# Gram products of an RWKV layer on four array tiles, with the transposes as identity products and a longer lead for their operands

## The chip, the core and the metric

One core of a Trainium2 chip runs the whole step: TensorE (PE, its weight loads as PEld), VectorE (DVE), ScalarE (ACT), GpSimd (POOL) and SyncE (SP), which issues most DMAs. The metric is device time in microseconds. The granted clock of TensorE has two levels, 1.2 and 2.4 GHz, shown as 0.5 and 1.0.

## What is computed

One inference step of a hybrid layer over 1024 latent and 256 context tokens: RMSNorm with adaptive modulation, one input projection, eight heads of differential attention, sixteen heads of a bidirectional RWKV-7 scan, gates, an output projection, a final RMSNorm. The part that the change touches is the scan, per head and direction:

```python
def step(S, inp):
    r_t, w_t, k_t, v_t, kk_t, b_t = inp
    sa = jnp.einsum('bhvk,bhk->bhv', S, -kk_t)
    S = S * w_t[:, :, None, :] + sa[..., None] * b_t[:, :, None, :] + v_t[..., None] * k_t[:, :, None, :]
    return S, jnp.einsum('bhvk,bhk->bhv', S, r_t)
```

## The kernel before

**Two stages.** First come the projections: 66 column blocks of 128, each over 1280 tokens in three pieces of 512, 512 and 256. `chunk` (L327 to L335) is one such piece: 24 matmuls (L331 to L333, the high and low parts of the split operands), one evacuation, and then one `next` on each generator in `active`, which is how all other work of this stage is handed out: one step of a generator per projection piece. Then comes the mixing stage (`mix_phase`), which runs the chunked scan, the attention and the output projection.

**The scan in chunks of 32 tokens.** For each pair of heads p (eight pairs, two heads of 64 channels on partitions 0 to 63 and 64 to 127) and each direction d, `b_k` calls `decays` and `weights` for the decay factors and then `products`, which goes through the 1280 tokens in five segments of eight chunks. For a segment, `operands` (L458 to L479) writes `ra` (DVE, L469 and L470), sends it to DRAM, and writes `bk` (DVE L474 and L475, POOL L476 to L478). `gram` (L440 to L456) then makes, for every chunk and head, the 64x64 Gram product of `bk` and `ra` (L446: 16 products, on the two array tiles on the diagonal, partitions 0 to 63 to outputs 0 to 63 and 64 to 127 to 64 to 127), masks it into `km` (DVE, L447), transposes `bk` with four 128x128 transposes (L450), copies these into `km` (ACT, four copies, L453) and sends `km` to DRAM array `kt` with two DMAs (L455). There are 8 x 2 x 5 = 80 such grams. An f32 product that is not a transpose shows as two matmul records in the trace, a transpose as one.

**Buffers.** `bk` and `km` have one buffer each, `ra` has two. The PSUM pool `psm` has four banks and serves all small products of the stage. A tile `wcs` of 2560 bytes per partition keeps chunk decays of all pairs until `b_inv` sends it to DRAM at the end.

**What sets the order.** A scheduler orders each engine's instructions by its own estimate of when their inputs are there, so a gram can stand later in PE's order than where the program issues it. Each engine then runs its order strictly. `products` issues gram c one segment behind its operands:

```python
        def products(p, d, r, k, kn, wx, td, ta):
            last = None
            for c0 in range(0, T // CH, NC):
                if last is not None:
                    gram(p, d, *last)
                last = operands(p, d, r, k, kn, wx, td, ta, c0)
                yield
                if c0 == 0:
                    yield
            gram(p, d, *last)
```

**Later places that the text speaks of.** After the last pair, `b_inv` inverts small triangular blocks on POOL (L731, L733); their result goes out by the DMA at L735. The mixing stage begins with a load of `wc` on POOL's queue (L838). In the mixing stage each step has products at L875 (four per lane, on two 32-column array tiles in turn) and at L916 (eight, on four 32-column tiles); in PE's order there is a place where the four of L875 stand ahead of the eight of L916. L643 makes 32 products with 128x32 array tiles, four tiles side by side over the same 128 rows, in the projection stage.

## Time and profile before

| | |
|---|---|
| median of three runs | 2570.79 us (2562.2 to 2574.7) |
| the profiled execution | 2570.32 us, of it a span of 2568.6 us |
| PE busy | 2399.3 us, 93% of the span |
| DVE, ACT, POOL busy | 1541.7, 1282.3, 1159.6 us |
| mean granted clock of TensorE | 0.959 |
| chain that ended last | PE 64%, DMA 14%, DVE 7%, POOL 5% |

The shares are means over both stages. The projection stage ends near 1238 us; a row of a stage tells more than a row of the whole span. Time that an engine spends idle counts only where nothing else is on the path.

### The profile page before, as it was taken

To read this page: it belongs to the slowest core of one execution; us is meant where nothing else is said; L and a number is where in the kernel's file an instruction comes from. 1 tells how busy PE (TensorE), PEld (TensorE's weight loads), DVE (VectorE), ACT (ScalarE), POOL (GpSimd) and SP (SyncE) were. 2 spreads that over 40 slices of the span, in tenths; PEclk is the share of its full clock that TensorE was granted. 3 is DMA by queue.
4 is the path that set the end of the run, shared out by engine and by line. 5 is a ranking of instruction groups with operands and counts; after the bars stand their busy time and mean duration, and the time that the engine had idled before them with its cause. 6 is when DMAs were issued, how large, how long until landed. Compare 5 with 4: busy or idle time off the path is not lost.

```text
span 2568.6 us, 61542 instructions
## 1 busy us (share of the span) xinstructions
PE 2399.3 (93%) x23907; PEld 1921.9 (75%) x23907; DVE 1541.7 (60%) x3304; ACT 1282.3 (50%) x2932; POOL 1159.6 (45%) x1705
## 2 busy tenths in 40 slices
PE   5999999999999999999799999899899999999976
PEld 4888888888888888787577777677677777777754
DVE  5666675546445655533477776456674667655568
ACT  3334443334334433321377776567665577555732
POOL 4244343242433433447457778567582122321245
PEclk9999999999999999999799989999898999999987
DMA  7455656565555564566979797977889777776583
GB/s 244 110 154 132 187 145 174 136 166 161 157 145 150 134 180 120 149 168 174 227 158 194 141 183 172 203 166 166 181 193 225 193 184 169 194 197 154 143 265 114
DMA packets 477092, 437.35 MB, mean 170 GB/s; under 512 B 157288, under 2 KB 392868, under 8 KB 471681
## 3 DMA queue, kind: packets, MB, share of 16 engines
q1 hardware_dynamic: 473008, 424.74, 66.2%
q0 software_dynamic: 2704, 8.16, 1.5%
q8 instruction: 188, 3.08, 0.5%
q14 instruction: 104, 0.84, 0.1%
q10 hardware_dynamic: 1088, 0.52, 0.1%
HBM read 258.82 MB, written 163.47 MB: 164 GB/s over the span
## 4 chain that ended last, share of the span: by engine, by line
PE 64%; DMA 14%; DVE 7%; POOL 5%; SPq 4%; issue 3%; ACT 3%; POOLq 0%; DVEq 0%; ACTq 0%
PE sc L1061 6%; PE po L1115 5%; PE bank L889 3%; PE pg L446 3%; PE pa L1100 3%; PE bank L875 3%; PE pso L1284 2%; PE pso L1285 2%; PE pso L1286 2%; PE yb L795 2%; PE yb L916 2%; PE ptk L450 2%; DMA y<-ys 1%; PE psg_v L331 1%; PE psg_v L332 1%
## 5 line engine op out<-in xcount | busy, mean ns | idle before, releaser
L1061 PE MATMUL sc<-ka,q 128*128 128x512 f32 (+1 forms) x832 | 288.4, 441 | 16.9 <-DVE pb L1064 12.1
L1072 ACT ACTIVATE pb<-pb,mn 128x1536 f32<-128x1536 f32 (+1 forms) x160 | 218.3, 1365 | 55.3 <-DVE pb L1064 53.5
L904 DVE TENSOR_TENSOR R<-bank,wc 64x128 f32<-64x128 f32 x608 | 174.7, 287 | 113.8 <-PE bank L889 90.5
L1064 DVE TENSOR_SCALAR_CACHE_REDUCE pb<-sc,mn 128x512 f32<-128x512 f32 x256 | 191.6, 748 | 79.8 <-PE sc L1061 70.8
L1115 PE MATMUL po<-vk,aT 128*128 128x128 f32 x1600 | 236.3, 286 | 0.9 <-ACT aT L1102 0.9
L1115 PEld LDWEIGHTS po<-vk,aT 128*128 128x128 f32 x1600 | 210.6, 195 | 19.8 <-ACT aT L1102 1.9
L879 ACT COPY R<-bank 32x128 f32<-32x128 f32 x640 | 164.5, 257 | 120.2 <-PE bank L875 99.9
L476 POOL TENSOR_SCALAR ta<-ta,ka 128x256 f32<-128x256 f32 x80 | 81.6, 1020 | 295.0 <-DVE bk L474 294.8
L453 ACT COPY km<-ptk 64x256 f32<-64x256 f32 x320 | 117.3, 367 | 185.6 <-PE ptk L450 160.6
L731 POOL TENSOR_TENSOR tmp<-aw,tt 128x31 f32<-128x31 f32 (+15 forms) x310 | 166.8, 538 | 74.4 <-DMA aw<-kt 27.8
L733 POOL TENSOR_TENSOR tt<-tt,tmp 128x31 f32<-128x31 f32 (+15 forms) x310 | 182.3, 588 | 18.1
L1092 DVE SCALAR_TENSOR_TENSOR pb<-pb,cc,pb 128x512 f32<-128x512 f32 (+1 forms) x208 | 169.9, 864 | 2.2
L1061 PEld LDWEIGHTS sc<-ka,q 128*128 128x128 f32 x832 | 136.2, 197 | 45.4 <-DVE pb L1064 15.9
L799 ACT COPY L<-yb 32x384 f32<-32x384 f32 x312 | 146.3, 469 | 43.3 <-PE yb L795 36.7
L447 DVE TENSOR_TENSOR km<-pg,msk 128x512 f32<-128x512 f32 x80 | 55.0, 687 | 176.3 <-PE pg L446 156.6
L889 PE MATMUL bank<-R,L 128*64 128x64 f32 x2560 | 150.2, 242 | 9.7 <-ACT R L879 7.2
L889 PEld LDWEIGHTS bank<-R,L 128*64 128x64 f32 x2560 | 107.2, 144 | 69.4 <-issue 25.3
L875 PE MATMUL bank<-R,L 96*32 96x64 f32 x2560 | 133.9, 234 | 15.9 <-DVE R L904 8.5
L1284 PE MATMUL pso<-wohi,ohi 128*128 128x512 f32 x320 | 136.2, 426 | 12.4 <-DVE y L1353 7.7
L1100 PE MATMUL pa<-ident,pb 128*128 128x128 f32 x800 | 134.4, 289 | 10.9 <-DVE acc L1278 7.1
L875 PEld LDWEIGHTS bank<-R,L 96*32 96x32 f32 x2560 | 87.8, 115 | 71.8 <-issue 29.9
L1102 ACT COPY aT<-pa 128x512 f32<-128x512 f32 (+1 forms) x208 | 116.4, 569 | 37.7 <-PE pa L1100 34.1
(355 smaller groups left out, 6446.1 us busy)
## 6 DMA issues: line engine op xcount, KB each, us to landing
kt<-km SPq DMA_DIRECT2D x160, 256.0 KB, 3.7
L<-kt SPq DMA_DIRECT2D x80, 512.0 KB, 6.8
acc<-acc SPq DMA_DIRECT2D x50, 512.0 KB, 3.9
ra<-ra SPq DMA_DIRECT2D x160, 128.0 KB, 2.6
L<-ra SPq DMA_DIRECT2D x80, 256.0 KB, 6.8
R<-vb SPq DMA_DIRECT2D x160, 64.0 KB, 6.9
y<-ys SPq DMA_DIRECT2D x76, 128.0 KB, 5.8
wa<-w_ada SPq DMA_DIRECT2D x8, 1024.0 KB, 10.7
```

Of the source, the lines that this page charges most:

```text
L731: e.tensor_tensor(mv, aw[:n, t, t + 1:CH].unsqueeze(2).broadcast_to([n, w, j]), tt[:n, t:t + 1, 0:j].broadcast_to([n, w, j]), op=ALU.mult)
L733: e.tensor_tensor(tt[:n, t + 1:CH, 0:j], tt[:n, t + 1:CH, 0:j], mv, op=ALU.add)
L875: nc.tensor.matmul(bank[x][u:u + 32, 64 * d:64 * d + 64], L[0:96, h, d, k, 96:128], R[0:96, k, d, 64 * h:64 * h + 64], start=True, stop=Tr ...
L889: nc.tensor.matmul(bank[x][64 * h:64 * h + 64, o_:o_ + 64], L[:, h, d, k, 0:64], R[:, k, d, 64 * h:64 * h + 64], start=True, stop=True, ti ...
L904: nc.vector.tensor_tensor(dst[:, :, hs], bank[x][hs, 256:384].rearrange("p (d v) -> p d v", d=2), wcs[p][hs, sg + 1, :, c:c + 1].broadcast ...
L1061: nc.tensor.matmul(sc, q[:, v, m, qc], ka[:, m, 0:kn], start=(v == 0), stop=(v == 1))
L1064: nc.vector.tensor_scalar(pm[:, c * 512:c * 512 + kn], sc, -0.125, mn[:, c - 1:c] if c else None, op0=ALU.mult, op1=ALU.min, accum_out=mn[ ...
L1072: nc.scalar.activation(v, v, AF.Exp, bias=mn[:, c:c + 1], scale=-1.0, accum_out=B["l3"][:, m, k:k + 1])
L1092: nc.vector.scalar_tensor_tensor(a, B["p"][1][:, v], B["cc"], a, op0=ALU.mult, op1=ALU.add)
L1100: nc.tensor.transpose(pt[:, t * P:(t + 1) * P], B["p"][0][:, 512 * c + t * P:512 * c + (t + 1) * P], ident)
L1115: nc.tensor.matmul(po, B["aT"][c][:, t * P:(t + 1) * P], vk[:, t, :], start=(c == 0 and t == 0), stop=(c == last and t == nt - 1))
L1284: nc.tensor.matmul(ps, ohi[:, k - k0, :], whi[:, k, c], start=(n == 0), stop=False)
```

## The change

Four things. (1) The 16 Gram products and four transposes of a gram become 32 products of 64x64: for each chunk and head one with the identity (this gives the transposed `bk`) and one with `ra`, both with the same weights. They run on all four 64x64 array tiles: the first four chunks (f = 0) on the diagonal tiles, the last four (f = 1) on the other two, with outputs in two PSUM banks `pg[0]` and `pg[1]`. The four products of a tile position stand in this order: tile (0,0) identity and Gram, tile (64,64) both, tile (0,64) both, tile (64,0) both. (2) The evacuation goes by halves f: two masked products on DVE, two copies on ACT over 128 partitions, four DMAs. (3) `bk` gets two buffers, and a gram is issued two segments behind its operands: the operands of segments 1 to 4 are issued one projection piece earlier, the grams at the same pieces as before. (4) `wcs` becomes a tile of 320 bytes per pair, sent to DRAM once per pair, and the one DMA in `b_inv` goes.

```diff
@@ -311,7 +311,7 @@
 
         pr = p1.enter_context(ExitStack())
         rp = pr.enter_context(tc.tile_pool(name="rp", bufs=1, side="right", reuse_waits="tile"))
-        wcs = rp.tile([P, 8, 5, 2, NC], F32, name="wcs")
+        wcs = {}
         cosT = ap.tile([P, TL], F32, name="cosT")
         sinT = ap.tile([P, TL], F32, name="sinT")
         rst = rp.tile([P, SEG], F32, name="rst")
@@ -427,7 +427,9 @@
             nc.scalar.activation(wx[:, :, 1 - d:1 - d + CH], tv, AF.Exp, scale=-0.5 * DECAY)
             nc.scalar.activation(td, td, AF.Exp, scale=0.5 * DECAY)
             wl = wx[:, :, CH * (1 - d)]
-            ws = wcs[:, p, :, d, :]
+            if d == 0:
+                wcs[p] = rp.tile([P, 5, 2, NC], F32, tag="wcs", name=f"wcs{p}", bufs=1)
+            ws = wcs[p][:, :, d, :]
             seg = wl[:, 0:32].rearrange("p (s c) -> p s c", c=NC)
             if d == 0:
                 nc.gpsimd.tensor_copy(ws[:, 1:5], seg)
@@ -435,25 +437,29 @@
             else:
                 nc.gpsimd.tensor_copy(ws[:, 1:5], seg[:, ::-1, ::-1])
                 nc.gpsimd.tensor_copy(ws[:, 0], wl[:, 32:40][:, ::-1])
+                nc.sync.dma_start(s["wc"][:, 10 * p:10 * p + 10, :], wcs.pop(p).rearrange("r i d c -> r (i d) c"))
             return wx
 
         def gram(p, d, it, c0, ra, bk):
             km = rp.tile([P, NC, P], F32, tag="km", name=f"km{p}{d}{c0}", bufs=1)
-            pg = psm.tile([P, NC, HD], F32, tag="psm", name=f"pg{p}{d}{c0}")
-            for c in range(NC):
+            hn = NC // 2
+            pg = [psm.tile([P, hn, P], F32, tag="psm", name=f"pg{p}{d}{c0}_{f}") for f in range(2)]
+            for c in range(hn):
+                for f in range(2):
+                    for h in range(2):
+                        hs, g = slice(64 * h, 64 * h + 64), 64 * (h ^ f)
+                        w = bk[hs, hn * f + c, :]
+                        for n, v in enumerate((ident[hs, hs], ra[hs, hn * f + c, :])):
+                            nc.tensor.matmul(pg[f][g:g + 64, c, 64 * n:64 * n + 64], w, v, start=True, stop=True,
+                                             tile_position=(64 * h, g))
+            for f in range(2):
+                fs = slice(hn * f, hn * f + hn)
+                nc.vector.tensor_tensor(km[:, fs, HD:P], pg[f][:, :, HD:P], msk[:, d:d + 1].broadcast_to([P, hn, HD]),
+                                        op=ALU.mult)
+                nc.scalar.copy(km[:, fs, 0:HD], pg[f][:, :, 0:HD])
                 for h in range(2):
-                    hs = slice(64 * h, 64 * h + 64)
-                    nc.tensor.matmul(pg[hs, c, :], bk[hs, c, :], ra[hs, c, :], start=True, stop=True)
-            nc.vector.tensor_tensor(km[:, :, HD:P], pg, msk[:, d:d + 1].broadcast_to([P, NC, HD]), op=ALU.mult)
-            pt = psm.tile([P, NC // 2, P], F32, tag="psm", name=f"ptk{p}{d}{c0}")
-            for c in range(0, NC, 2):
-                nc.tensor.transpose(pt[:, c // 2, :], bk[:, c:c + 2], ident)
-            for e in range(2):
-                for h in range(2):
-                    nc.scalar.copy(km[64 * h:64 * h + 64, e:NC:2, 0:HD], pt[64 * e:64 * e + 64, :, 64 * h:64 * h + 64])
-            for h in range(2):
-                nc.sync.dma_start(s["kt"][p, it, :, :, h, d].rearrange("f r y -> r f y"),
-                                  km[64 * h:64 * h + 64].rearrange("r (f c) x -> r f (c x)", f=2))
+                    g = 64 * (h ^ f)
+                    nc.sync.dma_start(s["kt"][p, it, f, :, h, d], km[g:g + 64, fs].rearrange("r c x -> r (c x)"))
 
         def operands(p, d, r, k, kn, wx, td, ta, c0):
             st = -1 if d else 1
@@ -462,7 +468,7 @@
             tk = slice(c0 * CH, (c0 + NC) * CH)
             v3 = lambda x: x[:, tk].rearrange("p (c t) -> p c t", t=CH)
             ra = rp.tile([P, NC, HD], F32, tag="ra", name=f"ra{p}{d}{c0}", bufs=2)
-            bk = rp.tile([P, NC, HD], F32, tag="bk", name=f"bk{p}{d}{c0}", bufs=1)
+            bk = rp.tile([P, NC, HD], F32, tag="bk", name=f"bk{p}{d}{c0}", bufs=2)
             rv, av = ra[:, ::st, 0:CH], ra[:, ::st, CH:HD][:, :, ::st]
             kv, bv = bk[:, ::st, 0:CH], bk[:, ::st, CH:HD][:, :, ::st]
             wv_ = wx[:, c0:c0 + NC]
@@ -479,15 +485,15 @@
             return (it, c0, ra, bk)
 
         def products(p, d, r, k, kn, wx, td, ta):
-            last = None
+            made = []
             for c0 in range(0, T // CH, NC):
-                if last is not None:
-                    gram(p, d, *last)
-                last = operands(p, d, r, k, kn, wx, td, ta, c0)
+                if len(made) == 2:
+                    gram(p, d, *made.pop(0))
+                made.append(operands(p, d, r, k, kn, wx, td, ta, c0))
                 yield
-                if c0 == 0:
-                    yield
-            gram(p, d, *last)
+            gram(p, d, *made[0])
+            yield
+            gram(p, d, *made[1])
 
         def b_k(p):
             rows = slice(p * P, (p + 1) * P)
@@ -655,9 +661,6 @@
         mix = []
 
         def b_inv():
-            nw = heads * 10
-            nc.sync.dma_start(s["wc"][:, 0:nw, :], wcs[:, 0:heads].rearrange("r p i d c -> r (p i d) c"))
-            yield
             aw = rp.tile([P, T], F32, tag="td", name="aw0")[:, 0:CH * CH].rearrange("p (t y) -> p t y", y=CH)
             tt = rp.tile([P, T], F32, tag="ta", name="tt0")[:, 0:CH * CH].rearrange("p (t y) -> p t y", y=CH)
             tmp = rp.tile([P, T], F32, tag="kn", name="tmp0")
```

The scheduler makes a new order from this. The first place is DVE in pair 2, direction 0 (names: `bk2016` is pair 2, direction 0, first chunk 16, so segment 2; `km200` the evacuation of the gram of segment 0). Before:

```order
L470 SCALAR_TENSOR_TENSOR ra208_4027<-s_k2_3703,pv_90,wx20_3862 128x8x32
L474 SCALAR_TENSOR_TENSOR bk200_3908<-ta20_3797,kn2_3868 128x8x32
L475 SCALAR_TENSOR_TENSOR bk200_3908<-bk200_3908,td20_3796 128x8x32
L164 TENSOR_TENSOR wlo_av1_3965<-w_av1_3962,whi_av1_3964 128x512
L358 SCALAR_TENSOR_TENSOR gb2_3969<-gb2_3969,psg_gb2_0_3970 128x512
L447 TENSOR_TENSOR km200_3997<-pg200_3998,msk_748 128x8x64
L469 TENSOR_TENSOR ra2016_4106<-s_r2_3317,wx20_3862 128x8x32
L470 SCALAR_TENSOR_TENSOR ra2016_4106<-s_k2_3703,pv_90,wx20_3862 128x8x32
L474 SCALAR_TENSOR_TENSOR bk208_4028<-ta20_3797,kn2_3868 128x8x32
L475 SCALAR_TENSOR_TENSOR bk208_4028<-bk208_4028,td20_3796 128x8x32
```

With the change:

```order
L480 SCALAR_TENSOR_TENSOR bk200_4172<-ta20_4060,kn2_4132 128x8x32
L480 SCALAR_TENSOR_TENSOR bk208_4209<-ta20_4060,kn2_4132 128x8x32
L481 SCALAR_TENSOR_TENSOR bk200_4172<-bk200_4172,td20_4059 128x8x32
L481 SCALAR_TENSOR_TENSOR bk208_4209<-bk208_4209,td20_4059 128x8x32
L164 TENSOR_TENSOR wlo_av1_4240<-w_av1_4237,whi_av1_4239 128x512
L358 SCALAR_TENSOR_TENSOR gb2_4244<-gb2_4244,psg_gb2_0_4245 128x512
L457 TENSOR_TENSOR km200_4272<-pg200_0_4273,msk_747 128x4x64
L457 TENSOR_TENSOR km200_4272<-pg200_1_4274,msk_747 128x4x64
L475 TENSOR_TENSOR ra2016_4315<-s_r2_3539,wx20_4125 128x8x32
L476 SCALAR_TENSOR_TENSOR ra2016_4315<-s_k2_3966,pv_90,wx20_4125 128x8x32
L480 SCALAR_TENSOR_TENSOR bk2016_4316<-ta20_4060,kn2_4132 128x8x32
L481 SCALAR_TENSOR_TENSOR bk2016_4316<-bk2016_4316,td20_4059 128x8x32
```

`bk` of segment 1 stood behind the evacuation of gram 0 and now stands ahead of it; behind that evacuation stands `bk` of segment 2.

The second place is POOL at the same segments (`suk1`, `uk1`: the rotary products of a key block, L583 and L584, after the change L589 and L590). Before:

```order
L478 TENSOR_TENSOR bk200_3908<-ta20_3797,td20_3796 128x8x32
L164 TENSOR_TENSOR wlo_av1_3965<-w_av1_3962,whi_av1_3964 128x512
L476 TENSOR_SCALAR ta20_3797<-ta20_3797,ka2_96 128x256
L477 TENSOR_TENSOR ta20_3797<-ta20_3797,s_k2_3703 128x256
L478 TENSOR_TENSOR bk208_4028<-ta20_3797,td20_3796 128x8x32
L583 TENSOR_TENSOR suk1_4038<-suk1_4038,sinT_746 128x1024
L584 TENSOR_TENSOR uk1_3835<-uk1_3835,cosT_745 128x1024
L476 TENSOR_SCALAR ta20_3797<-ta20_3797,ka2_96 128x256
L477 TENSOR_TENSOR ta20_3797<-ta20_3797,s_k2_3703 128x256
L478 TENSOR_TENSOR bk2016_4107<-ta20_3797,td20_3796 128x8x32
```

With the change:

```order
L484 TENSOR_TENSOR bk200_4172<-ta20_4060,td20_4059 128x8x32
L484 TENSOR_TENSOR bk208_4209<-ta20_4060,td20_4059 128x8x32
L164 TENSOR_TENSOR wlo_av1_4240<-w_av1_4237,whi_av1_4239 128x512
L482 TENSOR_SCALAR ta20_4060<-ta20_4060,ka2_96 128x256
L483 TENSOR_TENSOR ta20_4060<-ta20_4060,s_k2_3966 128x256
L484 TENSOR_TENSOR bk2016_4316<-ta20_4060,td20_4059 128x8x32
L589 TENSOR_TENSOR suk1_4326<-suk1_4326,sinT_745 128x1024
L590 TENSOR_TENSOR uk1_4098<-uk1_4098,cosT_744 128x1024
```

`bk` of segment 2 stood behind the two rotary products and now stands ahead of them; segment 3 now follows them.

The third place is PE at the gram of segment 0 of the same pair. Before:

```order
L333 MATMUL psg_gb2_0_3970<-hhi_97,wlo_gb2_3831 128x512
L446 MATMUL pg200_3998<-ra200_3907,bk200_3908 64x64 x16
L450 MATMUL ptk200_4016<-ident_78,bk200_3908 128x128 x4
L331 MATMUL psg_gb2_512_4049<-hhi_97,whi_gb2_3830 128x512
```

With the change (the eight products of one c; three more such groups follow):

```order
L333 MATMUL psg_gb2_0_4245<-hhi_97,wlo_gb2_4094 128x512
L453 MATMUL pg200_0_4273<-ident_78,bk200_4172 64x64
L453 MATMUL pg200_0_4273<-ra200_4171,bk200_4172 64x64
L453 MATMUL pg200_0_4273<-ident_78,bk200_4172 64x64
L453 MATMUL pg200_0_4273<-ra200_4171,bk200_4172 64x64
L453 MATMUL pg200_1_4274<-ident_78,bk200_4172 64x64
L453 MATMUL pg200_1_4274<-ra200_4171,bk200_4172 64x64
L453 MATMUL pg200_1_4274<-ident_78,bk200_4172 64x64
L453 MATMUL pg200_1_4274<-ra200_4171,bk200_4172 64x64
...
L331 MATMUL psg_gb2_512_4337<-hhi_97,whi_gb2_4093 128x512
```

The transposes are gone from their own place. In the new order every one of the 80 grams stands at the end of a projection piece, where the program issues it; before, the later grams of a pair stood up to 74 projection matmuls (counted in columns of 512) further back, and many inside a piece. Between the gram of segment 1 and that of segment 2 lies one piece of 256 tokens. The mixing stage has the same instructions in an order that differs in places.

## Rows read from the trace of the kernel before

**Rows 1.** Windows: us, busy time (instructions) by engine, clock, DMA share, GB/s.

```profile
150.00:1135.00 985.00, 962.03 (x7619) 812.96 (x7618) 552.17 (x848) 381.88 (x738) 374.48 (x421) 0.99 0.57 156
1135.00:1238.00 103.00, 96.17 (x579) 81.31 (x577) 35.08 (x50) 25.50 (x51) 68.74 (x80) 0.98 0.70 170
1238.00:2569.00 1331.00, 1220.46 (x14576) 928.93 (x14574) 866.10 (x2266) 820.58 (x2056) 665.28 (x1121) 0.93 0.78 181
```

**Rows 2.** Waits of PE, 150 to 1135 us: total us, times, longest us.

```profile
PE pg L446 <- POOL bk L478: 19.3, 12, 3.0
PE pg L446 <- DVE bk L475: 3.0, 2, 2.7
PE z L412 <- ACT w2h L509: 0.6, 1, 0.6
```

**Rows 3.** POOL's timeline, 396 to 411 us: start, duration, instruction, idle before it.

```profile
402.33 2.39 POOL L583 TENSOR_TENSOR suk<-suk,sinT 128x1024 f32<-128x1024 f32 x1 [5.86 <-ACT km L453]
404.67 2.60 POOL L584 TENSOR_TENSOR uk<-uk,cosT 128x1024 f32<-128x1024 f32 x1
407.25 1.59 POOL L476 TENSOR_SCALAR ta<-ta,ka 128x256 f32<-128x256 f32 x1
...
410.06 0.73 POOL L478 TENSOR_TENSOR bk<-ta,td 128x256 f32<-128x256 f32 x1
```

**Rows 4.** PE's timeline at the gram that waited for that `bk`.

```profile
410.84 1.15 PE L446 MATMUL pg<-ra,bk 64*64 64x64 f32 x32 [0.41 <-POOL bk L478]
```

**Rows 5.** Windows after the first and the last of five waited-for grams, columns of rows 1.

```profile
783.20:786.60 3.40, 3.40 (x11) 2.82 (x11) 3.01 (x7) 1.46 (x4) 1.95 (x2) 0.50 0.73 205
...
1104.10:1107.50 3.40, 3.40 (x11) 2.81 (x11) 1.80 (x4) 2.71 (x7) 1.33 (x1) 0.51 0.44 169
```

**Rows 6.** PE's timeline around one gram that waited for nothing, 517 to 520 us.

```profile
517.26 0.39 PE L332 MATMUL psg_gb<-hlo,whi_gb 128*128 128x512 f32 x1
517.49 0.39 PE L333 MATMUL psg_gb<-hhi,wlo_gb 128*128 128x512 f32 x1
517.81 1.15 PE L446 MATMUL pg<-ra,bk 64*64 64x64 f32 x32
518.88 0.66 PE L450 MATMUL ptk<-ident,bk 128*128 128x128 f32 x4
519.30 0.48 PE L331 MATMUL psg_gb<-hhi,whi_gb 128*128 128x512 f32 x1
```

**Rows 7.** PE's timeline in the mixing stage, two array tiles of L875 and others of L916.

```profile
1259.61 0.32 PE L875 MATMUL bank<-R,L 96*32 96x64 f32 x2
1259.64 0.32 PE L916 MATMUL yb<-R,L 128*32 128x64 f32 x1
1259.72 0.32 PE L875 MATMUL bank<-R,L 96*32 96x64 f32 x2
```

**Rows 8.** PE's timeline at 32 products on four tiles over the same rows.

```profile
501.12 0.76 PE L643 MATMUL pgt<-w_ada,pv 128*32 128x32 f32 x64
```

**Rows 9.** Groups by line, 0 to 1150 us: busy us, mean ns, idle before, releasers.

```profile
L453 ACT COPY km<-ptk 64x256 f32<-64x256 f32 x320 | 117.3, 367 | 185.6 <-PE ptk L450 160.6 <-DMA kt<-km 10.4 <-issue 5.8
L446 PE MATMUL pg<-ra,bk 64*64 64x64 f32 x2560 | 93.1, 223 | 22.3 <-POOL bk L478 19.3 <-DVE bk L475 3.0
L447 DVE TENSOR_TENSOR km<-pg,msk 128x512 f32<-128x512 f32 x80 | 55.0, 687 | 176.3 <-PE pg L446 156.6 <-DMA kt<-km 11.9 <-PE z L413 6.0
L469 DVE TENSOR_TENSOR ra<-s_r,wx 128x256 f32<-128x256 f32 x80 | 39.9, 498 | 4.4 <-ACT wx L427 4.3
```

**Rows 10.** Instructions on `km`: duration ns min/median/max; then its DMAs' us to landing.

```profile
L455 SPq DMA_DIRECT2D kt<-km x160: 574/581/1698, 153.9 to 1137.3; - x160
...
DMA to landing us min/median/max: 3.1/3.7/7.0
```

**Rows 11.** POOL's timeline between the stages.

```profile
1205.79 1.83 POOL L735 DMA_DIRECT2D td<-tt  x1 [0.30 <-POOL tt L733]
...
1237.30 0.60 POOL L838 DMA_DIRECT2D wc<-wc  x1 [21.11 <-PE psg_ga L333]
```

## The prediction

> **What bounds the kernel now.** I read the windows by stage first, then PE's waits in the projection stage, then the timeline around single grams. From 150 to 1135 us PE is busy 962 of 985 us at a granted clock of 0.99, while DVE has 552, ACT 382 and POOL 374 us of work [rows 1]: the stage is as long as PE's order. The 23 us that PE lacks are nearly all one wait: PE stood 22.3 us before grams because `bk` was late, 19.3 on POOL and 3.0 on DVE, 14 times; the next wait in the list is 0.6 us [rows 2]. The timeline shows how that comes about: POOL ran the two rotary products from 402.33 to 407.25 us, then the work on `ta`, and finished `bk` at 410.79 (410.06 and 0.73) [rows 3]; the gram on PE began at 410.84 [rows 4]. The stages follow each other through PE too: the mixing stage's first load on POOL's queue waited 21 us for the last projection, until 1237.30, and the inverse that it also needs had left POOL at 1205.79 [rows 11]. So time that PE saves in the projections moves the whole rest forward, until some 30 us of slack on POOL's side are used up, and POOL's inverse moves forward as well, since it follows the last operands.
>
> **The sum.** It is made against the profiled execution, 2570.3 us, of which 1.7 lie outside the span; the median of the runs is 2570.8, so it stands for both. A measurement of this kernel can tell about 0.5% (13 us) from no change.
>
> *The wait for `bk`.* The operands of segments 1 to 4 are issued one projection piece earlier, the grams at the same pieces. One piece is 24 matmuls, 0.23 us apart at 512 columns (517.26 to 517.49) [rows 6], so 5.5 us, half of that for the piece of 256 columns. The longest wait was 3.0 us [rows 2]. On DVE and POOL `bk` now stands ahead of what it used to stand behind, as the order shows. With the wait goes its echo: after five of these waits TensorE's clock stood at 0.50 (1.2 GHz) in a stretch of 3.4 us while PE was 3.4 us busy, of which I show the first and last [rows 5]. At half clock 3.4 us do 1.7 us of work: 5 x 1.7 = 8.5 us. Together 22.3 + 8.5 = 30.8 us, the most that this part can give. Segment 3 now stands behind the rotary products, and the piece before gram 2 is the short one, so I take five sixths: 26 us. The lower bound is nothing, if lateness only moves to other segments.
>
> *The products.* Before, a gram is 517.81 to 519.30 = 1.49 us on PE: 1.07 us for 32 records on two tiles, so 16 per tile, and 0.42 us for the transposes [rows 6]. After it is 64 records on four tiles, again 16 per tile, and no transposes. If the four tiles run side by side that is 1.07 us, the lower end. The question is whether they do, since now four records in a row belong to one tile. The nearest row is in the mixing stage: four products of L875 on two tiles stand ahead of those of L916; the first records of L875 began at 1259.61, L916 began on a third tile at 1259.64, and the next records of L875 only at 1259.72 [rows 7]. So PE passed eight records, most of them not begun, to reach a free tile in 0.03 us. The fourth tile here stands behind twelve records, 0.04 us by that rate, and some refilling comes on top: I take 1.14 us. Saved: 1.49 - 1.14 = 0.35 us, times 80 grams = 28 us (34 at 1.07). The Trainium skill has a rule against it: TensorE: Matmul & The Clock Gate, section Part 3: Packing small matmuls, says that matmuls start and end strictly in program order. By it the time would be that of the last rival below, and the rows above disagree with it. The same section says that a weight load overlaps running matmuls only on other row groups, which would keep the two tiles over the same rows apart. That too is not what the trace shows: 64 records on four tiles over the same 128 rows took 0.76 us, 12 ns each [rows 8]. The grams' records follow each other on one tile at 1.07/16 = 67 ns; those of L643 have half the columns, so one at a time I estimate 33 ns each, three times what the row has.
>
> *What lies beside.* ACT: 320 copies of 367 ns [rows 9] become 160 of the same 256 elements per partition, 59 us less of work that PE never waited for. DVE: 80 products of 687 ns become 160 of 128x256, at 498 ns by the nearest row [rows 9], 80 for 55 us: 25 us more, covered by 430 idle ones [rows 1]. SP: 320 issues for 160; at the old 0.58 us [rows 10] 93 us more, at half size perhaps nothing. Loads of the next projection's weights queue behind them on SP, but SP itself mostly waits for DVE and ACT at `km`, which now come as early. If that cover failed, PE would wait for weights; no such wait is in the list [rows 2]. `wcs` goes out in eight small DMAs off every path; the one in `b_inv` stood 30 us ahead of need [rows 11]. All this counts as nothing.
>
> *The mixing stage.* Same instructions, order changed in places, 1331 us long [rows 1]. I see no direction in it and give it no term, but half a percent either way (13 us) goes into the range.
>
> Sum: 2570.3 - 26 - 28 = **2516 us**.
>
> **Rivals.**
>
> *Two tiles at a time.* Tiles (0,0) and (64,0) put their outputs on the same PSUM partitions, in two banks. No row here shows two tiles of different rows sharing output partitions; if they took turns, the 64 records would need twice 1.07 = 2.14 us, 0.65 more than before, 52 us in 80 grams: 2570 - 26 + 52 = 2596 us, slower. This decides from a gram of 1.49 + 26/80 = 1.82 us on. For it speaks that nothing excludes it; against it, that all other pairings of tiles run together [rows 7, 8]. Chance 0.10.
>
> *A wait in place of the old one.* `km` has one buffer. Between gram 1 and gram 2 lies only the short piece, 2.8 us, and the gram, 1.1; but `km` is free only after its evacuation (about 1 us), four issues of up to 0.58 and 3.7 us to landing [rows 10], up to 7 us. DVE and ACT then stand up to 3 us with two of four PSUM banks full. PE feels it only if something else of `psm` needs a third and fourth bank in that time. If it does so in each of the 16 runs of five grams: 16 x 2.6 = 42 us, so 2558 us. An unlucky order of the mixing stage would end near the same value. Against it: before, DVE waited 11.9 us for this DMA [rows 9] and PE never for DVE there. Chance 0.14.
>
> *In program order.* If every record waited for the one before it on its own tile and the next tile could not pass, only each fourth record would overlap: 48 steps of 1.07/16 = 0.067 us, 3.2 us per gram, 1.7 more than before, 137 us: 2681 us. The rows of L875 and L916 speak against it [rows 7]. Chance 0.04.
>
> *Better than the sum.* All 30.8 us and 1.07 us per gram, a lucky mixing order: 2506 - 13 = 2493 us or less. Chance 0.06.
>
> **How the numbers follow.** The forecast itself has 0.66, with its own range of 2493 to 2540 (the two bounds above, and 13 us for the mixing stage on each side). The wait in its place has 0.14, some 0.04 of it under 2558. The range of 2490 to 2561 holds the forecast, half or more of that rival and part of the better case, some 0.78 in all; the two other rivals lie outside. Faster by more than 0.5% (under 2558): 0.66 + 0.06 + some 0.04 of the wait = 0.76. Slower (over 2583.6): 0.10 + 0.04 and a touch less for a mild form of the first rival: 0.12. Within 0.5%: the rest, 0.12.
>
> **What would show it.** Right: no wait of PE on `bk` over a few us in all; no window at 0.50 between 150 us and the end of the projections, or one or two; a gram of 64 records between two projection matmuls taking 1.07 to 1.2 us; the mixing stage's first load near 1185 us in place of 1237; ACT some 59 us less busy. Wrong: grams of 1.8 us or more, records of a gram going out in pairs of tiles, or PE waiting on ACT or DVE at `psm`. Wrong in the mixing stage: the load comes early, and the 1331 us after it have grown.

## The result, and the profile after

The change is slower: 2646.4 us against 2567.0 us for the kernel before, ratio 1.0316 [1.0265, 1.0367]. The profiled execution has a span of 2640.9 us, 72.3 more than before. The windows of the changed kernel, by stage (columns of rows 1; its projections end at 1282 us, before at 1237):

```profile
150.00:1135.00 985.00, 931.69 (x9560) 779.38 (x9559) 525.48 (x902) 305.65 (x561) 351.19 (x408) 0.97 0.57 149
1135.00:1282.00 147.00, 129.38 (x867) 109.14 (x858) 46.56 (x73) 32.44 (x64) 76.68 (x88) 0.92 0.67 169
1282.00:2640.00 1358.00, 1245.04 (x14597) 941.71 (x14595) 872.63 (x2267) 820.08 (x2058) 662.48 (x1122) 0.92 0.76 177
```

Against [rows 1], PE is busy 931.7 us of the 985 in place of 962.0, at a clock of 0.97 in place of 0.99: the projections lost time, and so did the mixing stage, 27 us longer. PE's waits in the same 985 us (total, times, longest), to be read beside [rows 2]:

```profile
PE pb L567 <- ACT km L459: 13.1, 5, 4.1
PE pg L453 <- POOL bk L484: 12.2, 5, 4.2
PE z L412 <- ACT km L459: 11.6, 6, 3.5
PE z L412 <- ACT w2h L515: 8.5, 2, 5.4
PE pg L453 <- DVE bk L481: 2.7, 1, 2.7
PE ptrva L379 <- ACT km L459: 2.3, 1, 2.3
```

The wait for `bk` (all waits at grams, `pg`) shrank from 22.3 to 16.3 us. The waits elsewhere rose from 0.6 to 37.0 us, the small ones included: products of other lines that take their banks from the same pool `psm` (`z` in `decays`, `pb` and `ptrva` for the value blocks) wait until ACT has emptied a gram's bank, or for `w2h`, a weight of `decays`. One of them in the timeline (start, duration, instruction, idle before it; `vb` are the values on their way to DRAM, `suk` is the swapped copy of a key block that the rotary products read):

```profile
922.92 0.36 PE L453 MATMUL pg<-ident,bk 64*64 64x64 f32 x8
...
924.71 0.70 ACT L459 COPY km<-pg 128x256 f32<-128x256 f32 x2 [1.09 <-DVE km L457]
...
929.86 0.36 PE L453 MATMUL pg<-ident,bk 64*64 64x64 f32 x8
...
929.87 3.84 SPq L583 DMA_DIRECT2D suk<-uk  x5
...
933.81 2.45 SPq L462 DMA_DIRECT2D kt<-km  x4
...
938.20 0.76 DVE L457 TENSOR_TENSOR km<-pg,msk 128x256 f32<-128x256 f32 x2 [6.92 <-DMA kt<-km]
938.70 0.66 ACT L459 COPY km<-pg 128x256 f32<-128x256 f32 x2 [8.14 <-DVE km L457]
...
939.13 1.22 PE L567 MATMUL pb<-rk,blk 128*128 128x256 f32 x2 [4.15 <-ACT km L459]
```

Read it from below. PE waited 4.15 us for a bank that ACT had not emptied; ACT stood behind DVE's half of the gram; DVE stood 6.92 us because `km` still held the gram of 922.92. That gram had been in `km` since 925.4, but its four transfers left SP only from 933.81, as SP had stood for the landing of `vb` (5.1 us) and issued five `suk` transfers first. So `km` was taken from 924.3 to 938.2, 14 us, and the next gram came after 6.9. Over the stage DVE stood 118.6 us for this transfer in 32 places (total, times, longest), before 11.9 [rows 9]:

```profile
DVE km L457 <- DMA kt<-km: 118.6, 32, 6.9
```

Stalls are followed by half clock (window, columns of rows 1):

```profile
937.90:944.70 6.80, 5.57 (x77) 5.05 (x78) 3.68 (x9) 1.99 (x4) 2.74 (x2) 0.50 0.86 174
```

By the trace's clock records, between 100 and 1180 us 58.0 us were at 0.50, before 17.1, and each of the twelve stretches at 0.50 begins within a wait of PE or up to 1.5 us behind one. At 0.50 the projection products of 512 columns follow each other every 427 ns, at 1.0 every 227, so nearly half of such a stretch is lost.

Of the products, the gram itself did get shorter (PE's timeline at a gram that waited for nothing, to set beside [rows 6]):

```profile
1012.24 0.39 PE L333 MATMUL psg_k<-hhi,wlo_k 128*128 128x512 f32 x1
1012.55 0.37 PE L453 MATMUL pg<-ident,bk 64*64 64x64 f32 x8
1012.72 0.32 PE L453 MATMUL pg<-ra,bk 64*64 64x64 f32 x8
...
1013.53 0.33 PE L453 MATMUL pg<-ra,bk 64*64 64x64 f32 x5
1013.79 0.50 PE L331 MATMUL psg_k<-hhi,whi_k 128*128 128x512 f32 x1
```

1012.55 to 1013.79 is 1.24 us in place of 1.49.

**The sum of the loss.** I mark three points in each trace: the end of the first 4400 of the 4752 projection products (L331 to L333; the start of the one that follows), the start of the last, and the start of the last matmul of all. Before they stand at 1155.3, 1236.8 and 2557.8 us, after at 1190.5, 1282.3 and 2630.4. Up to the 4400th 35 us were lost: waits grew by 53.3 - 22.9 = 30 us, half clock costs (58.0 - 17.1)/2 = 20 us more, and 80 grams give back 0.25 x 80 = 20 us, together 30 of the 35. The end of the projections lost another 10, the mixing stage 27 (204.8 us of it at half clock, before 177.5, which by the same halving is an estimated 13 of the 27).

### The profile page after: what moved, and what is told of

The parts are those of the page before. It is cut to its first block, busy times and chain, and to the rows that moved or that the text cites. A ratio compares the mean times of both kernels' runs of the same rounds, so it can differ in the third digit from the quotient of the medians.

```text
span 2640.9 us, 66066 instructions
## 1 busy us (share of the span) xinstructions
PE 2427.5 (92%) x26147; PEld 1929.5 (73%) x26147; DVE 1533.2 (58%) x3384; ACT 1212.5 (46%) x2772; POOL 1143.6 (43%) x1705
## 4 chain that ended last, share of the span: by engine, by line
PE 50%; DMA 19%; DVE 9%; SPq 8%; POOL 5%; issue 4%; ACT 4%; DVEq 0%; POOLq 0%; ACTq 0%
PE po L1118 5%; PE sc L1064 5%; PE pa L1103 3%; PE bank L892 3%; PE yb L798 2%; PE bank L878 2%; PE pg L453 2%; DMA y<-ys 2%; SPq L462 2%; PE pso L1287 2%; PE pso L1289 2%; DMA acc<-acc 2%; PE pso L1288 2%; DMA kt<-km 2%; PE yb L919 1%
## 5 line engine op out<-in xcount | busy, mean ns | idle before, releaser
L1064 PE MATMUL sc<-ka,q 128*128 128x512 f32 (+1 forms) x832 | 298.0, 449 | 15.3 <-DVE pb L1067 9.4
L1118 PE MATMUL po<-vk,aT 128*128 128x128 f32 x1600 | 242.1, 290 | 4.4 <-ACT aT L1105 4.2
L1095 DVE SCALAR_TENSOR_TENSOR pb<-pb,cc,pb 128x512 f32<-128x512 f32 (+1 forms) x208 | 175.2, 888 | 2.1
L1064 PEld LDWEIGHTS sc<-ka,q 128*128 128x128 f32 x832 | 138.0, 200 | 45.3 <-DVE pb L1067 13.7
L457 DVE TENSOR_TENSOR km<-pg,msk 128x256 f32<-128x256 f32 x160 | 60.6, 418 | 164.1 <-DMA kt<-km 134.0
L459 ACT COPY km<-pg 128x256 f32<-128x256 f32 x160 | 55.7, 373 | 213.4 <-DVE km L457 211.5
L1103 PE MATMUL pa<-ident,pb 128*128 128x128 f32 x800 | 137.4, 294 | 13.7 <-DVE acc L1281 7.3
```

Source lines behind the costliest of these rows:

```text
L1064: nc.tensor.matmul(sc, q[:, v, m, qc], ka[:, m, 0:kn], start=(v == 0), stop=(v == 1))
L1095: nc.vector.scalar_tensor_tensor(a, B["p"][1][:, v], B["cc"], a, op0=ALU.mult, op1=ALU.add)
L1103: nc.tensor.transpose(pt[:, t * P:(t + 1) * P], B["p"][0][:, 512 * c + t * P:512 * c + (t + 1) * P], ident)
L1118: nc.tensor.matmul(po, B["aT"][c][:, t * P:(t + 1) * P], vk[:, t, :], start=(c == 0 and t == 0), stop=(c == last and t == nt - 1))
```

## The experiments

All times are us. "4400th", "last" and "mixing" are the marks above, mixing counted from the last projection product to the last matmul; "bk", "other" are PE's waits at grams and elsewhere from 150 to 1135; "kt" is DVE's wait for the transfer out of `km` there (in e15 and e16 it is ACT that waits, 72 and 151); "half" the time at half clock from 100 to 1180. The marks and waits of a row come from one execution each, while the total times of one kernel's executions lie 8 to 30 us apart (the traced ones of e12, e16 and e17 lie 10 to 15 us above their median), so a difference of some 10 us between two marks is weak by itself. The scheduler's order changes with each edit too: with the lag (the change, e1, e3 to e8, e12 to e14, e16) the grams keep their places among the projection products to within a few, without it (before, e2, e9 to e11, e15, e17) they move from run to run. Such moves are counted below in projection products of 512 columns, as read from the order of the records.

```
                      median  ratio [interval]          4400th   last mixing   bk other    kt  half
before                2567.0                            1155.3 1236.8 1321.0 22.3   0.6  11.9  17.1
the change            2646.4  1.0316 [1.0265, 1.0367]   1190.5 1282.3 1348.1 16.3  37.0 118.6  58.0
e1  lag only          2603.7  1.0138 [1.0089, 1.0187]   1163.4 1246.6 1343.0  9.5  17.9  94.9  23.9
e2  products only     2609.7  1.0143 [1.0104, 1.0183]   1167.9 1250.4 1344.0 43.1   2.7  33.3  41.0
e3  kt in series      2706.4  1.0526 [1.0485, 1.0566]   1254.3 1345.8 1349.2 23.4  66.9 168.4 109.2
e4  tiles in turn     2620.6  1.0202 [1.0153, 1.0251]   1184.3 1272.2 1330.4 12.6  47.7 121.9  54.6
e5  two km            2633.0  1.0232 [1.0192, 1.0273]   1181.2 1271.3 1346.8 36.2  18.8   7.3  58.0
e6  control of e5     2646.1  1.0270 [1.0226, 1.0314]   1189.1 1279.2 1355.3 15.3  37.5 121.3  61.4
e7  lag, two km       2590.7  1.0064 [1.0043, 1.0085]   1150.0 1236.1 1344.0 12.9   6.9   1.1  17.1
e8  e1, old mixing    2582.4  1.0054 [1.0031, 1.0078]   1163.2 1255.1 1313.4 10.1  20.3  76.4  17.1
e9  four issues       2594.0  1.0099 [1.0071, 1.0127]   1156.3 1238.5 1344.2 21.2   3.7  22.4  13.7
e10 e2, kt by ACT     2567.8  0.9989 [0.9972, 1.0006]   1147.7 1236.1 1324.7 23.1   6.6  29.2  27.3
e11 before, kt by ACT 2557.3  0.9954 [0.9932, 0.9975]   1146.2 1226.7 1317.5 17.2   0.2   4.8  10.2
e12 change, kt by ACT 2640.2  1.0265 [1.0224, 1.0307]   1198.3 1288.3 1352.3 10.7  48.0  93.2  64.9
e13 e5, kt by ACT     2606.0  1.0134 [1.0105, 1.0162]   1162.9 1249.8 1338.5 16.8  22.9   1.2  36.3
e14 e8, kt by ACT     2599.5  1.0089 [1.0054, 1.0124]   1170.4 1265.5 1327.0 14.6  14.0  80.1  34.1
e15 e2, ACT first     2606.3  1.0152 [1.0118, 1.0186]   1166.1 1252.1 1339.2 40.1   1.8    -   47.8
e16 change, ACT first 2651.1  1.0328 [1.0284, 1.0371]   1201.2 1291.1 1357.1 10.2  54.6    -   61.4
e17 e10, tiles in turn 2595.2 1.0109 [1.0069, 1.0149]   1158.7 1237.4 1360.9 36.5   9.8  16.3  37.5
```

### The two halves of the change apart

**e1**, the change with the old `gram` (old products, two transfers per gram):

```diff
-  the new gram (L442 to L462)
+  the old gram (L444 to L456 of the kernel before)
```

> The old Gram products with the new order (operands two segments ahead, two bk buffers, wcs per pair). Theory K (the new gram holds its one km buffer too long: four issues on SP in place of two, so DVE and ACT stand for the transfer and PE for them): the loss goes with the new products, so here DVE's wait for the kt transfer is near the 22 us of before (under 40), PE hardly waits at z or pb, the wait for bk is mostly gone, and the last projection is near 1237 - 26 = 1211 us (1200 to 1225). Theory L (the lag itself piles DVE's and POOL's work up at the wrong places): the waits of PE at z, pb and w2h stay as with the change, and the last projection is at 1250 us or later. The mixing stage has another order again: 1331 us or up to 30 us off either way.

The last projection came at 1246.6, between the theories. The wait for `bk` went down to 9.5 as hoped, but DVE stood 94.9 us for `kt`, with two issues per gram. So theory K is wrong in blaming the four issues: the lag alone makes the transfer late. The distances of the grams go with it: before, the median within a run of five was 9.4 us from one gram's first record to the next's (7 of 67 under 8 us), in e2 9.0 (16 of 64), here 7.1 (53 of 64), in the change 6.9 (49 of 64). With one `bk` and the short lead the scheduler had set the grams further back in PE's order and so further apart, and `km` had come free meanwhile.

**e2**, the new gram with the old `products` and one `bk`:

```diff
-  bk = rp.tile(..., bufs=2);  grams two segments behind
+  bk = rp.tile(..., bufs=1);  grams one segment behind
```

> The new Gram products with the old order (one bk buffer, operands one segment ahead, wcs per pair). Theory K: DVE's wait for the kt transfer is over 80 us as with the change, PE waits at z and pb 20 us or more, beside about 20 us for bk as before: last projection at 1270 to 1300 us. Theory L: no such waits, only those for bk: last projection near 1237 - 28 + 8 = 1217 us (1205 to 1235).

Neither: `kt` stays at 33, the waits at z and pb at 2.7, but the wait for `bk` doubled to 43.1 and half clock more than doubled to 41.0. A shorter gram can reach the next one's operands earlier and wait for them longer, but two other things differ from the kernel before: 63 of the 80 grams stand earlier in PE's order, by 6 projection products on average, and SP issues four transfers in place of two. e10 has the same products and waits 23.1 us. So how much of the 43.1 comes from the shorter gram is not shown.

**e4**, the order of the products (e4 is the change):

```diff
-  for f: for h: for n (identity, ra): product
+  for n (identity, ra): for (f, h) in (0,0),(0,1),(1,0),(1,1): product
```

> The change, with the products issued so that the tile changes from each to the next (all four identity products of a column block, then the four others) and so each weight loaded twice in a row never. If the order of the products is what makes a gram last 1.23 us on PE where 1.07 was the lower end, a gram falls to 1.07 to 1.12 us and the projections gain 9 to 13 us; if PE's rate over 64 records is the limit, it stays at 1.23 or grows. By theories K and L alike the waits at z, pb and for the kt transfer stay (over 80 us for the latter).

As expected where the order is the limit. PE's timeline at a gram:

```profile
1007.84 0.34 PE L453 MATMUL pg<-ident,bk 64*64 64x64 f32 x8
1008.00 0.30 PE L453 MATMUL pg<-ra,bk 64*64 64x64 f32 x8
...
1008.70 0.30 PE L453 MATMUL pg<-ra,bk 64*64 64x64 f32 x8
1008.93 0.50 PE L331 MATMUL psg_k<-hhi,whi_k 128*128 128x512 f32 x1
```

1.09 us from first record to the next projection product, 80 x 0.144 = 11.5 us less in all. No gram has moved against the change, so this is the cleanest test of a shorter gram: by its trace 6 us of the 11.5 reach the 4400th product and 10 the last. Most of the 26 us in the median is the mixing stage, which has a new order (1330.4).

### The `km` buffer

**e3** was to join the four transfers of a gram into two:

```diff
-  for f, h: dma_start(kt[p, it, f, :, h, d], km[g:g + 64, fs])
+  for n: dma_start(<both f, strided>, km[64 * n:64 * n + 64])
```

> The change, with the four kt transfers of a gram joined into two of 256 KB (one for each half of the partitions). Theory K: SP issues 160 where it issued 320, at 0.58 us each; km comes free some 1.2 us earlier per gram, DVE's wait for the transfer falls from 119 us to under 70, PE's waits at z and pb from 27 us to under 12, and the last projection comes at 1225 to 1260 us in place of 1282. Theory L: as with the change, 1275 to 1290 us.

A miss that served as the opposite experiment: SP waited for one transfer of `km` to land before it issued the next (I take it that the strided destinations counted as overlapping):

```profile
SPq L463 <- DMA kt<-km: 111.5, 67, 3.9
```

With it `km` was held longer, DVE's wait rose to 168 us, PE's other waits to 67, half clock to 109, and the 4400th product came 64 us later.

**e5**, and **e6** as its control:

```diff
-  los = one tile for each b, d;   km: bufs=1
+  los = one tile for each d, used for both b;   km: bufs=2   (e6: bufs=1)
```

The space for the second buffer comes from leaving out the low-rank input of the iclr products, which read that of the decay; e7 and e13 leave out the same.

> The change with two km buffers; the space for the second comes from leaving out one part of the computation: the iclr products read the decay's low-rank input, of which one copy is kept in place of both. The order on every engine is that of the change. Theory S (grams that no longer wait for bk stand 6.9 us apart where they stood 9 us apart before, less than the time for which one km is held, so DVE stands for the kt transfer with everything behind it, and PE for DVE and ACT): DVE's wait for kt falls from 119 to under 15 us, PE's waits at z and pb from 27 to under 6, the time at half clock up to the end of the projections from 58 to under 30, and the last projection comes at 1282 - 45 = 1237 us or earlier (1205 to 1240). Theory T (the transfers on SP are late in themselves, as the four issues keep the loads of w2 and of the weights back): PE's waits for w2h and for the weights stay, and the last projection is at 1260 us or later. The mixing stage keeps its order, so by the theory that the order makes its length it stays at 1348 us (1340 to 1356); if it was long because the projections ended badly, it falls back to 1321 to 1330.

> The control of the run before: the same space is freed by leaving out the same part (the iclr products read the decay's low-rank input), but km keeps one buffer. All theories: as with the change, 2646 us, last projection at 1282, within 10 us.

e6 is the change, as it should be. In e5 the wait for `kt` is gone (7.3), yet only 8 us of the projections came back (1189.1 to 1181.2): the wait moved to `bk`, 36.2 us in six places. One of them in e5's timeline, DMA queue, POOL, DVE and PE:

```profile
395.34 3.92 SPq L583 DMA_DIRECT2D suk<-uk  x5
399.35 2.46 SPq L462 DMA_DIRECT2D kt<-km  x4
401.91 1.26 SPq L478 DMA_DIRECT2D ra<-ra  x2
403.22 2.81 SPq L583 DMA_DIRECT2D suk<-uk  x3
...
408.01 2.39 POOL L589 TENSOR_TENSOR suk<-suk,sinT 128x1024 f32<-128x1024 f32 x1 [13.40 <-DMA suk<-uk]
...
412.73 1.23 DVE L610 TENSOR_TENSOR uk<-uk,suk 128x1024 f32<-128x1024 f32 x1 [10.85 <-POOL uk L590]
...
417.95 0.52 PE L453 MATMUL pg<-ident,bk 64*64 64x64 f32 x8 [8.07 <-POOL bk L484]
```

The last three `suk` transfers stand behind four of `kt` and two of `ra` on SP; POOL's rotary products wait for them, DVE for POOL with a segment's operands behind, and PE 8.07 us for those. In the kernel before the same products began at 402.33 [rows 3]. So theories S and T each hold a part. The mixing stage kept its length, 1346.8.

**e7**, e1 with two `km` and the same freed space:

> The old Gram products with the new order and two km buffers, the space again from the iclr products reading the decay's low-rank input. Theory S: DVE's wait for kt falls from 95 to under 15 us, PE's waits at z, pb and ptrva from 15 to under 3, and the last projection comes at 1247 - 25 = 1222 us (1208 to 1228): what the lag alone was to give. Theory T: 1240 us or later. Mixing stage 1343 us as with the lag alone if its order makes its length.

The `kt` wait is gone and 13 us came back (1163.4 to 1150.0), but the lag's best case is 5 us ahead of the kernel before at the 4400th product, not 26, and nothing at the last one.

### The mixing stage

**e8** is e1 with one number changed:

```diff
-  if n % 8 == 0: yield      (b_inv)
+  if n % 12 == 0: yield
```

> The lag alone with one km buffer, as in the run of the lag alone, and one number more: the inverse's steps are handed out twelve at a time in place of eight, by which every engine's order in the mixing stage (but for a few of SP's) becomes that of the kernel before. Theory M (the length of the mixing stage hangs on the order that the scheduler gives it, and any other order than before's costs 10 to 28 us): projections end at 1247 us as with the lag alone, the mixing stage takes 1321 us (1316 to 1328), total 2575 us. Theory N (the mixing stage is longer because the projections end differently): it takes 1335 us or more again.

Theory M holds. The two mixing stages as windows, e1 first:

```profile
1246.60:2589.50 1342.90, 1247.42 (x14593) 945.11 (x14593) 866.23 (x2250) 820.91 (x2054) 668.32 (x1122) 0.93 0.77 178
```

```profile
1255.10:2568.50 1313.40, 1213.63 (x14595) 923.60 (x14593) 862.35 (x2250) 819.45 (x2054) 667.27 (x1122) 0.94 0.79 182
```

The same instructions, and PE idle for 95 and 100 us; what differs is that PE is busy 34 us longer with them in the one order (191.1 us at half clock in e1, 153.6 in e8, so an estimated 18 of the 34 are the clock). Over all runs, the order of the kernel before (the same sequence on DVE, ACT and POOL in the traces) took 1313 to 1327 us (before, e8, e10, e11, e14), the change's own 1338 to 1357 (the change, e3, e5, e6, e12, e13, e16), the other orders 1330 to 1361. What in an order costs the time was not found.

### The queue of the transfers

**e9**, the kernel before with its transfers halved:

```diff
-  for h: dma_start(kt[p, it, :, :, h, d], km[64 * h:64 * h + 64])
+  for f, h: dma_start(kt[p, it, f, :, h, d], km[64 * h:64 * h + 64, 4 * f:4 * f + 4])
```

> The kernel before with one thing changed: each of a gram's two kt transfers of 256 KB is issued as two of 128 KB, so SP issues 320 in place of 160. Old products, old lag. Theory Q (an issue holds SP for 0.58 us whatever its size; 160 more of them push back what stands behind them on SP, the suk transfers first, with them POOL's rotary products and then bk): PE's wait for bk rises from 22 to over 32 us, the time at half clock up to 1180 us from 17 to over 30, and the last projection comes at 1250 to 1268 us. Theory P (the loss comes from the new products, their two PSUM banks and their evacuation): as before, 1233 to 1243 us. The mixing stage has another order: 1330 to 1350 by theory M.

Theory Q is not borne out: with 160 more issues the projections end where they did (1156.3, 1238.5). The scheduler set 51 of the 80 grams later here, 5 projection products on average, which may hide a small cost. Nearly all of e9's 1% is its mixing order, 23 of 25 us.

**e10** (e2) and **e11** (the kernel before) with the transfers issued by ACT:

```diff
-  nc.sync.dma_start(s["kt"]...
+  nc.scalar.dma_start(s["kt"]...
```

> The new products with the old lag (one bk buffer), and the four kt transfers issued by ACT behind its own copies in place of SP. The order of the mixing stage is that of the kernel before on all engines. Theory Q: PE's wait for bk falls to 25 us or less, half clock up to 1180 us under 25, the products give their 0.25 to 0.35 us per gram, and the last projection comes at 1217 us (1208 to 1228); with 1321 us of mixing 2551 us in all, faster than the kernel before. Theory P: as with the new products alone, 1245 to 1255 us.

> The kernel before, its two kt transfers per gram issued by ACT in place of SP, nothing else; mixing order that of the kernel before. Theory Q: SP has 160 issues less, suk comes earlier, PE's wait for bk falls from 22 to 10 to 16 us and the last projection comes at 1224 to 1233 us. Theory P: no change, 1233 to 1240 us.

With `kt` off SP the 4400th product came 20 us earlier with the new products (1167.9 to 1147.7) and 9 with the old ones. With e9 this says that it is hardly the number of issues. I take it that it is SP's standing for `km` with everything else behind it, 207 us in the kernel before:

```profile
SPq L455 <- DVE km L447: 141.7, 53, 8.2
...
SPq L455 <- ACT km L453: 65.7, 56, 2.2
```

This was not tried by itself, and the order moved as well (60 grams in e11, by up to 30 projection products; 57 in e10, by up to 9), so the queue's own share is not shown. e11 is the fastest kernel measured, 0.46% (0.25 to 0.68) under the kernel before. e10 lost its 8 us again at the end of the projections: PE waited 9.9 us there in place of 6.4, and 13.7 us were at half clock in place of 3.4. One of these waits, 3.7 us, is at L798, products that stand in PE's order before the last projections and need the inverse:

```profile
1209.18 1.18 PE L798 MATMUL pp<-L,Tb 32*32 32x96 f32 x23 [3.71 <-DMA Tb<-td]
```

**e12** to **e14** do the same to the change, to e5 and to e8:

> The change with its four kt transfers per gram issued by ACT behind its copies in place of SP; one km buffer; mixing order that of the change. If the queue is a cause beside the km buffer: DVE's wait for kt falls from 119 to 60 to 95 us, since the issue no longer stands behind SP's other work, PE's 4400th projection product comes at 1165 to 1180 us in place of 1190, and the total is 2615 to 2632 us (mixing 1348 as with the change). If the queue does not matter here: 1186 us or later and 2640 us.

> The change with two km buffers and with kt issued by ACT; the space again from leaving out one part (the iclr products read the decay's low-rank input). Both suspected costs are away. If these two are the whole loss: DVE's wait for kt under 15 us, PE's wait for bk under 20, half clock up to 1180 us under 30, and the 4400th projection product at 1125 to 1140 us, 20 us or so ahead of the lag with two km buffers (1150), which is the products' saving. If the operands' chain (suk transfers, rotary products on POOL, bk) sets the pace by itself: bk waits of 25 us or more and 1145 to 1165 us. Mixing 1348 us in both cases.

> The old products with the lag, kt issued by ACT, one km buffer, the inverse's steps handed out twelve at a time so that the mixing order is that of the kernel before. If the lag gives what it was made for once km comes free earlier: DVE's wait for kt under 50 us, PE's wait for bk under 8, the 4400th projection product at 1138 to 1146 us, and the total 2545 to 2556 us, no slower than the kernel before with kt on ACT (2557). If the end of the projections hangs on the inverse (PE waited 11.7 us for its result in the run with this order and kt on SP): the last projection stays at 1240 to 1255 us and the total at 2560 to 2580.

e12 and e14 are misses; by the medians e12 takes as long as the change. With one `km` the late issue became ACT's own stall: the issues take ACT 0.6 us each, and ACT then stands for the transfer with the work of other lines behind it, 89 us in all, where the change has no such wait. The largest of these waits:

```profile
ACT u_k L352 <- DMA kt<-km: 32.5, 13, 3.3
```

The issues in e12:

```profile
L462 ACTq DMA_DIRECT2D kt<-km x300: 452/608/2223, 153.2 to 1110.5; - x150
```

e13 lies at the bad end of its range: with both suspected costs away the 4400th product comes 28 us earlier than in the change, but 13 later than with the old products in e7 (waits of PE 39.6 us in place of 19.8, half clock 36.3 in place of 17.1).

### Where the products' saving went

**e15** (on e2) and **e16** (on the change) take away ACT's wait for DVE at each bank:

```diff
-  DVE: km[.., HD:P] = pg[f][.., HD:P] * msk;  ACT: km[.., 0:HD] = pg[f][.., 0:HD]
+  ACT: km[:, fs] = pg[f];  DVE: km[.., HD:P] *= msk
```

> The new products with the old lag (as in e2: one km buffer, kt on SP), but ACT alone copies each whole bank (256 plus 256 columns), and DVE then masks its half in place in km. If ACT's wait for DVE at each bank is what eats the products' saving: ACT's wait for DVE at km (246 us in e2) is gone, PE's wait for bk falls from 43 to under 28 us, half clock from 41 to under 28, and the 4400th projection product comes at 1143 to 1156 us in place of 1168. If not: 1160 us or later.

> The change with the same evacuation (ACT copies each bank, DVE masks in km). If the wait of ACT for DVE is a cause: PE's waits at z, pb and ptrva for ACT's km (27 us) fall under 12, half clock from 58 to under 45, and the 4400th projection product comes at 1165 to 1180 us in place of 1190, total 2615 to 2630. If the km buffer's hold sets the pace whoever comes first: 1185 us or later, the waits as before, total 2640 or more. Mixing 1348 in both.

Neither gained: 1166.1 and 1201.2. In e16 the grams stand where they stand in the change, and the waits stay, so there it is not the cause who empties the bank first. e15 says less, since 67 of its grams stand earlier than in e2, by 7.5 projection products on average.

**e17** is e10 with the order of e4:

> New products with the tiles in turn, old lag, one km and one bk buffer, kt issued by ACT. If PE's time still sets the pace there: a gram takes 1.09 us on PE, and the 4400th projection product comes 80 x 0.144 = 11 us before that of the run with the first order, at 1134 to 1141 us. If the operands' chain sets the pace, PE's waits for bk grow by as much: 1144 to 1150 us. The mixing order is a new one, so 1330 to 1350 us there, and the total lies between 2550 and 2590 us in either case.

It fell past both: 1158.7, 11 us later than e10 where a faster PE should have been 11 earlier. The waits at grams grew from 23.1 to 36.5 us and half clock from 27.3 to 37.5. So the time taken from PE was more than made up by waits and the clock. But this is no clean price of a shorter gram: the scheduler set 63 of the 80 grams later than in e10, by 5 projection products on average, and the traced execution lies 15 us above the kernel's median. In e4, where no gram moved, half of the same saving and more came through.

## Why the prediction was wrong

**The premise, "the stage is as long as PE's order".** It held for the order as it was. PE was 98% busy because the scheduler had let the grams drift to where `bk` was nearly ready. The margin was not PE's alone: set against the kernel with the old products and the same queue (e2 against before, e10 and e17 against e11), 20 to 32 us of work less on PE came back as waits and half clock, in orders that had moved too. Of e4's 11.5 us, with the grams at the same places, 6 to 10 came through. 430 idle us of DVE [rows 1] were no cover, since the chain of DVE, POOL, SP and ACT is late in places, not on average.

**The wait for `bk`, -26.** The sum gave the operands one piece more, 5.5 us, because the grams stay "at the same pieces". That is where they are issued. In PE's order they stood 35 projection products (0.23 us each) behind those places on average, up to 74, and with the change they stand at them: the grams came forward by 8 us on average where the operands gained 5.5. The wait fell by 6 us in the change. With the lag alone it fell by 13, and with `km` out of the way (e7) everything together gave 5.

**The products, -28.** The four tiles do run side by side; "two at a time" and "program order" fell. The size was off by a little: 1.24 us, not 1.14, since four records in a row on one tile do cost something; in turn they take 1.09 (e4). One after the other, at the 67 ns of [rows 6], 64 records would take 4.3 us. The Trainium skill's rule (TensorE: Matmul & The Clock Gate, Part 3: Packing small matmuls) that products start and end strictly in order is not what this trace shows for four tiles: in PE's order every two identity products have a Gram product between them, and at 1012.55 eight identity records start before the first Gram record. But the 20 us saved, in place of 28, did not shorten the stage in the change.

**What lies beside, "counts as nothing".** This step failed most, and with it the sign that the prediction set for itself came up, PE waiting on ACT at `psm`. The `kt` transfer was counted by its issue time; what counted was that `km` has one buffer, that SP serves in order, and that DVE and ACT stand for both. "SP itself mostly waits for DVE and ACT at km, which now come as early" was half of it: what SP has in front of a `kt` issue can hold it 8 us (925.4 to 933.81).

**The rival "a wait in place of the old one".** The right mechanism with its price cut short: I gave it 2.6 us once in each run of five grams and a hold of up to 7 us. DVE stood for the transfer in 32 places, the hold was up to 14 us, and the echo in the clock was left out (20 us). A second buffer gave 8 us back in e5, 13 in e7 and 35 in e13 (against e12).

**The mixing stage, +-13.** "I see no direction in it": the stage grew by 27 us, and by e8 and the runs with the same orders this goes with its order. The same order repeats its length within 14 to 19 us, so it could have been taken as an unknown with its own, wider bound; the kernel before has the best order of those seen. The forecast's own range does not come out of its sum either: with the wait at nothing, its stated lower bound, the sum is 2542 us before the 13 for this stage, not 2540 with them.

**The slack of 30 us at the inverse.** It was read from L838 [rows 11]. PE already waited for the inverse earlier, at L795, 1.3 us in the kernel before and 11.7 in e8:

```profile
PE pp L795 <- DMA Tb<-td: 1.3, 1, 1.3
...
PE pp L795 <- DMA Tb<-td: 11.7, 1, 11.7
```

So the slack was about nothing: in these orders the last projections stand behind products that need the inverse.

What stays open: why the new products with two `km` and `kt` on ACT (e13) are 13 us behind e7, and what a shorter gram is worth where the scheduler moves the grams. Separate banks for ACT's and DVE's half on four tiles were not tried, as two tiles would write the same partitions of one bank.

## What to carry to other kernels

An engine that is busy 98% of a stage is not proof that its work sets the pace: if its instructions stand where the scheduler found their operands ready, work taken out can come back as waits; try it by shortening that work alone, and look whether the order stayed. Before operands are made earlier, look at what the lateness kept apart, and count for every tile that has one buffer the time from its first write to the landing of its transfer, with all that stands ahead of the issue on its queue. Where a scheduler sets the order, measure an edit with the untouched stage's order held fixed, or the differences between its orders (here 1313 to 1361 us) hide the edit.

## What had not been expected of the hardware

Four 64x64 tiles with records in turn took 1.09 us for 64 records, with four in a row on one tile 1.24. Half clock followed the waits closely: in the runs of the table the time at 0.50 (1.2 GHz in place of 2.4) is 0.55 to 1.2 times PE's waits, and nearly half of it is lost (427 ns a product in place of 227), so that by this estimate a microsecond waited in the projections cost 0.3 to 0.6 more. And one line that moved the transfers from SP to ACT (e11) gained 9 us up to the 4400th product: the Trainium skill (DMA: Bandwidth & Descriptors, Issuing engines are not separate DMA queues) says that this saves only the issuing sequencer's time; SP issued 160 transfers less there, but e9, with 160 more, lost nothing. What the gain came from, what stands behind a late transfer on SP or the moved order, is not separated here, and in e12 there was no gain.
